# Layer 1's attention scores: the second pass of the query split contracts 64 rows instead of 128, in five PSUM banks at once

## The chip, the cores and the metric

The kernel runs on one core of a Trainium2 chip. The metric is the device time of one execution in microseconds. Before the change the median of three runs is 1772.62 us (1768.93 to 1773.08).

## What is computed

The reference is a two-layer backbone over 1024 latent tokens and 256 context tokens of width 1024. Layer 0 is a latent attention, layer 1 a differential attention. The change lies in layer 1, of which this matters:

```python
q, k, v, gate = project(h, True)          # 8 heads, each with 2 maps of 64 columns
q_c, k_c, v_c, gate_c = project(h_c, False)
...
s = jnp.einsum('bqhgd,bkhd->bhgqk', qb, k).astype(jnp.float32) * scale   # per map; k is latent and context keys, 1280
p = jax.nn.softmax(s, axis=-1).astype(v.dtype)
return jnp.einsum('bhgqk,bkhv->bqhgv', p, v)
...
o = o1 - lam_full.astype(o1.dtype) * o2   # map 0 minus a multiple of map 1
```

Each head has two attention maps, 0 and 1. Each map's scores contract only 64 numbers per query and key. Both maps share the same values of 128 columns.

## The kernel before, in words

Layer 0 and the passage to layer 1 come first and are not touched. Layer 1 runs head after head, eight heads, and within a head over eight tiles of 128 queries. One call of `step1` is one such tile; the text calls it a step and numbers the steps 0 to 63, so step 31 is the last tile of head 3.

TensorE (PE) runs in the order in which the code is written (`manual_schedule` for PE). The orders of VectorE (DVE), ScalarE (ACT), GpSimd (POOL) and the DMA queue (SP) are set by the framework's scheduler from dependences, priorities and its own estimates of time. Every engine works its own list strictly in that order.

One step issues on PE: the scores of its tile (`scores1`), then, in slices between the rest, projections for the next head (`some(side, ...)`, lines 186 to 188), the product with the values of the tile two steps back (`values1`, lines 1392 to 1394), and transposes of the joined map of the tile one step back (`turn1`, line 1384) in three groups of four, four and two.

The numbers are fp32 split in two fp16 parts, high and low. For each map m, `KS[m]` holds 128 rows: the 64 rows of the key's high part and below them the 64 rows of its low part. `QS[m]` holds the query's high part twice, one copy under the other, so one matmul over 128 rows gives (high key + low key) times high query. `Q1[m]` holds the query's low part twice in the same way, and a second matmul over 128 rows adds (high key + low key) times low query. So a block of 512 scores takes two matmuls of 512 columns, lines 1348 and 1349.

`scores1` handles five banks of PSUM in turn: first the context block, where 256 columns of map 0 and 256 of map 1 share a bank; then two blocks of 512 for map 0; then, after a slice of projections, two blocks of 512 for map 1. All of layer 1's PSUM is one ring of eight banks (tag "b"), given out in the order of the code: a bank is written again when the tile that had it eight grants earlier has been read.

What follows a step's scores outside PE:

- DVE reduces each bank to a row maximum: line 1361 the context bank, line 1365 each block of 512. Line 1367 combines three of them to the negative maximum of a map, `mx`. It is needed before any exponential of that map.
- ACT takes the exponentials, three per map (line 1371: 512, 512 and 256 columns), from PSUM to `p0` or `p1`, with the row sums in `sm`. `p0` has two buffers, `p1` one.
- DVE adds the sums (line 1374), forms the factor (1375, 1376) and joins the maps, `p0 + factor * p1` over 1280 columns (line 1377).
- In the next step PE transposes the joined map, ACT writes the high part of it (`ph`, line 182) and DVE the low part (`pl`, line 183).

`prod_k1` and `prod_q1` make the next head's keys and queries. Their tails (`fin`) split the numbers and move them by SP's DMA queue into the 64-row halves of `KS`, `QS` and `Q1`: for a head four transfers for the keys, and eight for each of the two halves of the queries. `wx`, `wy`, `uw`, `kH` and `kL` in the traces belong to this preparation of the next head.

The last head (steps 56 to 63) has no next head to prepare; its slices are filled with the output projection of the layer.

Of the kernel before, what the change touches and what calls it, by code (L numbers as in the profile page):

```python
# [11 lines left out]
F16 = mybir.dt.float16  # L12
# [42 lines left out]
def hybrid_kernel(  # L55
# [30 lines left out]
    def dmv(dst, src):  # L86
        sp.dma_start(dst, src)
# [962 lines left out]
    with ow_ctx, spool("o0") as op0:  # L1050
# [96 lines left out]
        for t in range(8):  # L1147
# [48 lines left out]
            "pl": ([P, NT, P], F16, 2), "KS0": ([P, NTOK], F16, 2), "KS1": ([P, NTOK], F16, 2),  # L1196
            "QS0": ([P, SEQ], F16, 2), "QS1": ([P, SEQ], F16, 2), "Q10": ([P, SEQ], F16, 2),
            "Q11": ([P, SEQ], F16, 2), "vh": ([P, NT, P], F16, 2), "vl": ([P, NT, P], F16, 2),
            "o1": ([P, P], F32, 3), "o2": ([P, P], F32, 2), "mx": ([P, 8], F32, 2), "sm": ([P, 8], F32, 4),
# [6 lines left out]
    TAGO = {"res": ([P, D], F32, 2), "z": ([P, D], F32, 2), "gb3": ([P, D], F32, 1),  # L1206
            "bs": ([P, 2, 6], F32, 2), "mv": ([P, 4], F32, 2)}
    for k_, v_ in TAGL.items():
        rot(wl, v_[0], v_[1], k_, v_[2], first=True)
# [38 lines left out]
    def prod_k1(h, made=()):  # L1248
# [14 lines left out]
        def fin():  # L1263
            H, L = w1("kH"), w1("kL")
            split16(H, L, kr, kc1)
            for m in range(2):
                r = slice(m * HD, m * HD + HD)
                dmv(ks[m][:HD, :], H[r, :])
                dmv(ks[m][HD:, :], L[r, :])

# [3 lines left out]
    def prod_q1(h, b, ps=None):  # L1274
# [64 lines left out]
    def scores1(h, t):  # L1339
# [6 lines left out]

        def st_of(out, m, c0, n):
            pe.matmul(out, qs[m][:, ts], ks[m][:, c0:c0 + n], start=True, stop=False)  # L1348
            pe.matmul(out, q1[m][:, ts], ks[m][:, c0:c0 + n], start=False, stop=True)  # L1349

        st = {}

        def chunk(c0, ms):
            n = 512 // len(ms)
            st[c0, ms] = b = bank("b")
            for i, m in enumerate(ms):
                st_of(b[:, i * n:(i + 1) * n], m, c0, n)
            return b

        b = chunk(SEQ, (0, 1))  # L1360
        dve.tensor_reduce(mx[:, 0:2], b.rearrange("p (a b) -> p a b", a=2), axis=AX.X, op=ALU.max, negate=True)  # L1361
        for m in range(2):
            for i, c0 in enumerate((0, 512)):
                b = chunk(c0, (m,))
                dve.tensor_reduce(mx[:, 2 + 2 * m + i:3 + 2 * m + i], b, axis=AX.X, op=ALU.max, negate=True)  # L1365
            nb = mx[:, 6 + m:7 + m]
            dve.tensor_scalar(nb, mx[:, 2 * m + 2:2 * m + 3], mx[:, 2 * m + 3:2 * m + 4], mx[:, m:m + 1],  # L1367
                              op0=ALU.min, op1=ALU.min)
            for i, (c0, n, b) in enumerate(((0, 512, st[0, (m,)]), (512, 512, st[512, (m,)]),
                                            (SEQ, CTX, st[SEQ, (0, 1)][:, m * CTX:(m + 1) * CTX]))):  # L1370
                act.activation(p[m][:, c0:c0 + n], b, AF.Exp, bias=nb,  # L1371
                               accum_out=sm[:, 2 + 3 * m + i:3 + 3 * m + i])
            yield
# [344 lines left out]
```

## Time and profile before

| What | Value |
|---|---|
| runs, device time | 1773.08, 1772.62, 1768.93 us; median 1772.62 us |
| profiled execution, span from first to last instruction | 1767.7 us (its own device time is not among the numbers; the three runs lie 1.3 to 5.4 us above this span) |
| mean granted TensorE clock | 0.993 |
| busy in the span | PE 94%, weight loads 70%, DVE 69%, ACT 63%, POOL 46% |
| layer 1's steps 0 to 56, 947.70 to 1606.31 us | PE busy 623.01, DVE 521.04, ACT 460.95, POOL 221.44 of 658.61 us |
| PE's first scores, line 1348 | 947.6 us |
| scores on PE, 947 to 1720 us | line 1348 126.5 us, line 1349 129.7 us busy, 384 matmuls each |

How to read it: a busy share is an average; an engine that is busy 94% of the time need not be the one that others wait for. So the chain of waits is read beside it: the view that goes back from the last instruction, at each step to whatever released it. A matmul's row begins when it is issued and includes the time until its last result is written, so rows of consecutive matmuls overlap, and the distance from one start to the next is what a matmul takes from PE.

### The profile page before, as it was taken

What the parts mean: (1) busy time and instruction counts of PE and PEld (TensorE: products, weight loads), DVE (VectorE), ACT (ScalarE), POOL (GpSimd) and SP (SyncE); (2) the same over time, 40 slices, a digit from 0 to 9 for tenths busy, and PEclk for the clock granted to TensorE, in tenths of its full rate; (3) what the DMA queues carried; (4) which work ended last, traced back from release to release, by engine and by line L of the source; (5) the groups of instructions that cost most, each with busy time, mean ns of one, the idle gap of its engine ahead of it and who ended that gap; (6) DMA issues with size and microseconds to landing.
All of it is one profiled execution on the core that took longest, in us unless ns stands there. A gap on an engine that the chain in (4) does not pass through costs nothing. (4 is left out here: it accounts for less than half of the span.)

```text
span 1767.7 us, 36788 instructions
## 1 busy us (share of the span) xinstructions
PE 1660.4 (94%) x14564; PEld 1231.8 (70%) x14564; DVE 1224.6 (69%) x2037; ACT 1118.5 (63%) x2235; POOL 821.9 (46%) x740
## 2 busy tenths in 40 slices
PE   7999989999999998899999999999999999987998
PEld 6999956556666655577867676767676767666876
DVE  7658666565565666646856778787878787878664
ACT  3551177777777778845635676767676767758542
POOL 1432147667767776845552323241424233354454
PEclk9999999999999999999999999999999999999999
DMA  8258520110111122245522222231212222142331
GB/s 308 81 152 259 166 68 21 43 44 22 42 46 25 39 57 62 65 168 196 167 96 64 80 68 80 67 81 55 60 51 63 60 58 75 32 125 66 112 108 72
DMA packets 111225, 154.84 MB, mean 88 GB/s; under 512 B 13415, under 2 KB 84679, under 8 KB 111054
## 3 DMA queue, kind: packets, MB, share of 16 engines
q1 hardware_dynamic: 102654, 144.90, 27.3%
q10 hardware_dynamic: 8400, 7.61, 1.3%
q8 instruction: 114, 1.87, 0.4%
q14 instruction: 57, 0.47, 0.1%
HBM read 98.65 MB, written 27.07 MB: 71 GB/s over the span
## 5 line engine op out<-in xcount | busy, mean ns | idle before, releaser
L780 POOL TENSOR_TENSOR pl<-p,ph 128x1024 f16<-128x1024 f32 (+1 forms) x176 | 364.3, 2076 | 148.4 <-ACT ph L779 122.6
L1371 ACT ACTIVATE p<-ps_b,mx 128x512 f32<-128x512 f32 (+1 forms) x384 | 230.2, 617 | 58.9 <-DVE mx L1367 57.4
L778 ACT ACTIVATE p<-ps_a,esc 128x1024 f32<-128x1024 f32 (+1 forms) x176 | 189.0, 1074 | 94.8 <-PE ps_a L836 88.8
L760 DVE TENSOR_REDUCE mx<-ps_a 128x1 f32<-128x1024 f32 x128 | 155.3, 1222 | 129.9 <-PE ps_a L758 129.8
L779 ACT CAST ph<-p 128x1024 f16<-128x1024 f32 (+1 forms) x176 | 177.1, 1006 | 5.5
L1365 DVE TENSOR_REDUCE mx<-ps_b 128x1 f32<-128x512 f32 x256 | 164.9, 680 | 0.7 <-PE ps_b L1349 0.7
L849 PE MATMUL ps_d<-Vh,pl 128*128 128x65 f16 x1344 | 146.0, 194 | 4.4 <-POOL pl L780 4.4
L846 PE MATMUL ps_d<-Vh,ph 128*128 128x65 f16 x1344 | 148.2, 195 | 0.0
L848 PE MATMUL ps_d<-Vl,ph 128*128 128x64 f16 x1344 | 147.0, 193 | 0.0
L846 PEld LDWEIGHTS <-ph 128*128 128x128 f16 x1344 | 123.3, 97 | 18.1 <-issue 4.9
L848 PEld LDWEIGHTS <-ph 128*128 128x128 f16 x1344 | 124.0, 98 | 12.2 <-issue 0.3
L1348 PE MATMUL ps_b<-KS,QS 128*128 128x512 f16 (+1 forms) x384 | 126.5, 347 | 5.9 <-DVE pl L183 2.9
L1349 PE MATMUL ps_b<-KS,Q 128*128 128x512 f16 (+1 forms) x384 | 129.7, 347 | 0.0
L834 PE MATMUL ps_a<-qH,KH 100*128 100x512 f16 x320 | 121.9, 381 | 7.8 <-ACT p L778 3.5
L1396 POOL TENSOR_TENSOR sm<-sm,us 128x1 f32<-128x1 f32 x64 | 18.5, 289 | 234.3 <-DVE sm L1375 221.2
L849 PEld LDWEIGHTS <-pl 128*128 128x128 f16 x1344 | 123.2, 97 | 5.8 <-POOL pl L780 5.8
L1384 PE MATMUL ps_b<-idr,p 128*128 128x128 f32 x640 | 103.8, 278 | 24.2 <-ACT p L1371 6.2
L183 DVE SCALAR_TENSOR_TENSOR pl<-ps_b,lcf,ph 128x512 f16<-128x512 f32 (+1 forms) x192 | 116.9, 653 | 11.2 <-ACT ph L182 11.2
L182 ACT ACTIVATE ph<-ps_b,lcf 128x512 f16<-128x512 f32 (+1 forms) x192 | 115.2, 647 | 13.9 <-PE ps_b L1384 13.8
L835 PE MATMUL ps_a<-qH,KL 96*128 96x512 f16 x320 | 121.8, 381 | 0.0
L836 PE MATMUL ps_a<-qL,KH 96*128 96x512 f16 x320 | 121.2, 379 | 0.0
L1384 PEld LDWEIGHTS ps_b<-idr,p 128*128 128x128 f32 x640 | 78.2, 143 | 49.0 <-ACT p L1371 11.6
(438 smaller groups left out, 5290.7 us busy)
## 6 DMA issues: line engine op xcount, KB each, us to landing
ws<-in_dw SPq DMA_DIRECT2D x28, 512.0 KB, 3.9
adw<-in_ada_w SPq DMA_DIRECT2D x24, 512.0 KB, 4.6
adaw<-in_ada_w SPq DMA_DIRECT2D x16, 512.0 KB, 7.3
g<-sg_d SPq DMA_DIRECT2D x16, 512.0 KB, 8.5
sg_d<-gg ACTq DMA_DIRECT2D x40, 128.0 KB, 3.6
o_d<-op SPq DMA_DIRECT2D x7, 640.0 KB, 3.8
xt<-in_xT SPq DMA_DIRECT2D x16, 256.0 KB, 4.4
wgs<-in_w_in SPq DMA_DIRECT2D x32, 128.0 KB, 3.1
```

Source lines behind the costliest of these rows:

```text
L760: dve.tensor_reduce(mx[:, t, 0:1], ps, axis=AX.X, op=ALU.max)
L778: act.activation(p32[:, :n], st, AF.Exp, scale=esc0)
L779: act.copy(ph[:, :n], p32[:, :n])
L780: pool.tensor_tensor(pl[:, :n], p32[:, :n], ph[:, :n], op=ALU.subtract)
L846: pe.matmul(pv[:, t, :], ph[:, ts], Vh[:, k, h, :], start=(k == kcs[0] and t == 0), stop=False, skip_group_check=True)
L848: pe.matmul(pv[:, t, :V0], ph[:, ts], Vl[:, k, h, :], start=False, stop=False, skip_group_check=True)
L849: pe.matmul(pv[:, t, :], pl[:, ts], Vh[:, k, h, :], start=False, stop=(k == NT - 1), skip_group_check=True)
L1348: pe.matmul(out, qs[m][:, ts], ks[m][:, c0:c0 + n], start=True, stop=False)
L1349: pe.matmul(out, q1[m][:, ts], ks[m][:, c0:c0 + n], start=False, stop=True)
L1365: dve.tensor_reduce(mx[:, 2 + 2 * m + i:3 + 2 * m + i], b, axis=AX.X, op=ALU.max, negate=True)
L1371: act.activation(p[m][:, c0:c0 + n], b, AF.Exp, bias=nb, accum_out=sm[:, 2 + 3 * m + i:3 + 3 * m + i])
L1384: pe.transpose(st[:, j * P:(j + 1) * P], pc[:, (k0 + j) * P:(k0 + j + 1) * P], idn)
```

## The change

The low part of the query is kept once, as one tile of 128 rows (`QL`, map 0 in rows 0 to 63, map 1 in rows 64 to 127), in place of two copies for each map. The second pass contracts 64 rows: low query times high key only. The product of low query and low key, of the size of the split's own rounding, is left out. To make the rows meet, `KS[1]` now has its low part above and its high part below. Map 0's second matmul then uses rows 0 to 63 of the array, map 1's rows 64 to 127, and the two follow each other, each into its own bank.

For the context block a second form of the high key (`kctx`, one per head in turn) is kept: 512 columns, map 0's keys in the upper left, map 1's in the lower right, zeros elsewhere. One matmul of 512 columns with `QL` gives both maps' low-query products for the context.

To have pairs, `scores1` first issues the first pass of all blocks, into all five banks, then the four second passes; map 1's block comes first in each pair. The slice of projections that stood between map 0 and map 1 now comes after all scores. The maxima and exponentials are written in the code in the same grouping as before, with the context bank's maximum behind map 0's two. The transfers of the low query are gone (four for each half of a head's queries), its split writes `QL` directly, and two transfers per head fill `kctx`, which POOL zeroes once before layer 1.

```diff
-            "QS0": ([P, SEQ], F16, 2), "QS1": ([P, SEQ], F16, 2), "Q10": ([P, SEQ], F16, 2),
-            "Q11": ([P, SEQ], F16, 2), "vh": ([P, NT, P], F16, 2), "vl": ([P, NT, P], F16, 2),
+            "QS0": ([P, SEQ], F16, 2), "QS1": ([P, SEQ], F16, 2), "QL": ([P, SEQ], F16, 2), "vh": ([P, NT, P], F16, 2), "vl": ([P, NT, P], F16, 2),
...
+    kctx = [wl.tile([P, 2 * CTX], F16, name=f"kctx{i}") for i in range(2)]
+    for x in kctx:
+        pool.memset(x, 0.0)
...
             for m in range(2):
                 r = slice(m * HD, m * HD + HD)
-                dmv(ks[m][:HD, :], H[r, :])
-                dmv(ks[m][HD:, :], L[r, :])
+                o = slice(HD - m * HD, 2 * HD - m * HD)
+                dmv(ks[m][r, :], H[r, :])
+                dmv(ks[m][o, :], L[r, :])
+                dmv(kctx[h % 2][r, m * CTX:(m + 1) * CTX], H[r, SEQ:])
...
-            qt1[h] = [w1(f"Q1{m}") for m in range(2)], [w1(f"QS{m}") for m in range(2)]
+            qt1[h] = w1("QL"), [w1(f"QS{m}") for m in range(2)]
...
-            H, L = w1("kH")[:, :n], w1("kL")[:, :n]
+            H, L = w1("kH")[:, :n], q1[:, c]
...
-                dmv(q1[m][:HD, c], L[r, :])
-                dmv(q1[m][HD:, c], L[r, :])
...
-        def st_of(out, m, c0, n):
-            pe.matmul(out, qs[m][:, ts], ks[m][:, c0:c0 + n], start=True, stop=False)
-            pe.matmul(out, q1[m][:, ts], ks[m][:, c0:c0 + n], start=False, stop=True)
...
-        b = chunk(SEQ, (0, 1))
-        dve.tensor_reduce(mx[:, 0:2], b.rearrange("p (a b) -> p a b", a=2), axis=AX.X, op=ALU.max, negate=True)
+        def first(out, m, c0, n):
+            pe.matmul(out, qs[m][:, ts], ks[m][:, c0:c0 + n], start=c0 < SEQ, stop=c0 == SEQ, skip_group_check=True)
+
+        def second(out, m, c0, n):
+            r = slice(m * HD, m * HD + HD)
+            pe.matmul(out, q1[r, ts], ks[m][r, c0:c0 + n], start=False, stop=True, skip_group_check=True)
+
+        b = bank("b")
+        st = {(m, SEQ): b[:, m * CTX:(m + 1) * CTX] for m in range(2)}
+        pe.matmul(b, q1[:, ts], kctx[h % 2], start=True, stop=False, skip_group_check=True)
+        for m in range(2):
+            first(st[m, SEQ], m, SEQ, CTX)
+        for c0 in (0, 512):
+            for m in range(2):
+                st[m, c0] = bank("b")
+                first(st[m, c0], m, c0, 512)
+        for c0 in (0, 512):
+            for m in (1, 0):
+                second(st[m, c0], m, c0, 512)
         for m in range(2):
             for i, c0 in enumerate((0, 512)):
-                b = chunk(c0, (m,))
-                dve.tensor_reduce(mx[:, 2 + 2 * m + i:3 + 2 * m + i], b, axis=AX.X, op=ALU.max, negate=True)
+                dve.tensor_reduce(mx[:, 2 + 2 * m + i:3 + 2 * m + i], st[m, c0], axis=AX.X, op=ALU.max, negate=True)
+            if m == 0:
+                dve.tensor_reduce(mx[:, 0:2], b.rearrange("p (a b) -> p a b", a=2), axis=AX.X, op=ALU.max, negate=True)
             nb = mx[:, 6 + m:7 + m]
...
-            for i, (c0, n, b) in enumerate(((0, 512, st[0, (m,)]), (512, 512, st[512, (m,)]),
-                                            (SEQ, CTX, st[SEQ, (0, 1)][:, m * CTX:(m + 1) * CTX]))):
-                act.activation(p[m][:, c0:c0 + n], b, AF.Exp, bias=nb,
+            for i, (c0, n) in enumerate(CHUNKS):
+                act.activation(p[m][:, c0:c0 + n], st[m, c0], AF.Exp, bias=nb,
```

The added code shifts line numbers: the first passes are line 1350 in the changed kernel, the second passes line 1354, the context matmul line 1358, the maxima lines 1370 and 1372, the negative maximum line 1374, the exponentials line 1377, the sums and the join lines 1380 to 1383.

How PE's order moves is shown for step 31. In the names `ps_b` is a bank, `KS0` and `KS1` are the keys of the two maps, `QS` the high query, `Q10` the low query of map 0. Before, PE issues for map 0's two blocks, and what follows them:

```order
L1348 LDWEIGHTS QS0_2396_15894
L1348 MATMUL ps_b_2720_17920<-KS0_2377_15781,QS0_2396_15894 128x512
L1349 LDWEIGHTS Q10_2394_15892
L1349 MATMUL ps_b_2720_17920<-KS0_2377_15781,Q10_2394_15892 128x512
L1348 LDWEIGHTS QS0_2396_15894
L1348 MATMUL ps_b_2721_17924<-KS0_2377_15781,QS0_2396_15894 128x512
L1349 LDWEIGHTS Q10_2394_15892
L1349 MATMUL ps_b_2721_17924<-KS0_2377_15781,Q10_2394_15892 128x512
L186 LDWEIGHTS h1H_11336
L186 MATMUL ps_b_2722_17934<-wx_2596_17162,h1H_11336 128x256
```

After, the last two first passes and the four second passes of the same step stand like this:

```order
L1350 LDWEIGHTS QS0_2385_15850
L1350 MATMUL ps_b_2706_17849<-KS0_2369_15744,QS0_2385_15850 128x512
L1350 LDWEIGHTS QS1_2386_15851
L1350 MATMUL ps_b_2707_17851<-KS1_2370_15745,QS1_2386_15851 128x512
L1354 LDWEIGHTS QL_2384_15849
L1354 MATMUL ps_b_2705_17847<-KS1_2370_15745,QL_2384_15849 128x512
L1354 LDWEIGHTS QL_2384_15849
L1354 MATMUL ps_b_2704_17845<-KS0_2369_15744,QL_2384_15849 128x512
L1354 LDWEIGHTS QL_2384_15849
L1354 MATMUL ps_b_2707_17851<-KS1_2370_15745,QL_2384_15849 128x512
L1354 LDWEIGHTS QL_2384_15849
L1354 MATMUL ps_b_2706_17849<-KS0_2369_15744,QL_2384_15849 128x512
```

A bank was finished by the matmul right behind its first; now each block waits for its second pass behind all first passes, and the projections of line 186 come after the four second passes.

DVE's order moves with it, since the scheduler places the maxima anew. In step 31, `pl` is the low part of the tile one step back, `mx` the maxima. Before:

```order
L183 SCALAR_TENSOR_TENSOR pl_2708_17847<-ps_b_2714_17895,lcf_87,ph_2707_17846 128x256
L1361 TENSOR_REDUCE mx_2715_17910<-ps_b_2719_17914 128x2
L1365 TENSOR_REDUCE mx_2715_17910<-ps_b_2720_17920 128x1
L1365 TENSOR_REDUCE mx_2715_17910<-ps_b_2721_17924 128x1
L1367 TENSOR_SCALAR mx_2715_17910<-mx_2715_17910 128x1
L1365 TENSOR_REDUCE mx_2715_17910<-ps_b_2723_17947 128x1
L1365 TENSOR_REDUCE mx_2715_17910<-ps_b_2724_17951 128x1
L1367 TENSOR_SCALAR mx_2715_17910<-mx_2715_17910 128x1
L1374 TENSOR_REDUCE sm_2716_17911<-sm_2716_17911 128x2
```

After:

```order
L1372 TENSOR_REDUCE mx_2699_17837<-ps_b_2703_17841 128x2
L183 SCALAR_TENSOR_TENSOR pl_2692_17774<-ps_b_2698_17822,lcf_87,ph_2691_17773 128x256
L1370 TENSOR_REDUCE mx_2699_17837<-ps_b_2705_17847 128x1
L1370 TENSOR_REDUCE mx_2699_17837<-ps_b_2704_17845 128x1
L1370 TENSOR_REDUCE mx_2699_17837<-ps_b_2706_17849 128x1
L1370 TENSOR_REDUCE mx_2699_17837<-ps_b_2707_17851 128x1
L1374 TENSOR_SCALAR mx_2699_17837<-mx_2699_17837 128x1 x2
L1380 TENSOR_REDUCE sm_2700_17838<-sm_2700_17838 128x2
```

The first negative maximum stood behind three maxima; now both stand behind all five.

In step 33, the second tile of head 4, `p0` with two sources is the join of the step before. Before:

```order
L1361 TENSOR_REDUCE mx_2761_18216<-ps_b_2765_18220 128x2
L1376 SCALAR_TENSOR_TENSOR sm_2737_18074<-sm_2737_18074,nlam_86 128x1
L1365 TENSOR_REDUCE mx_2761_18216<-ps_b_2766_18226 128x1
L1377 SCALAR_TENSOR_TENSOR p0_2738_18075<-p1_2739_18076,sm_2737_18074,p0_2738_18075 128x1280
L1365 TENSOR_REDUCE mx_2761_18216<-ps_b_2768_18244 128x1
L1365 TENSOR_REDUCE mx_2761_18216<-ps_b_2767_18230 128x1
L1365 TENSOR_REDUCE mx_2761_18216<-ps_b_2769_18248 128x1
L1367 TENSOR_SCALAR mx_2761_18216<-mx_2761_18216 128x1 x2
```

After:

```order
L1372 TENSOR_REDUCE mx_2745_18141<-ps_b_2749_18145 128x2
L1381 RECIPROCAL sm_2721_18000<-sm_2721_18000 128x2
L1370 TENSOR_REDUCE mx_2745_18141<-ps_b_2751_18151 128x1
L1382 SCALAR_TENSOR_TENSOR sm_2721_18000<-sm_2721_18000,nlam_86 128x1
L1370 TENSOR_REDUCE mx_2745_18141<-ps_b_2753_18155 128x1
L1383 SCALAR_TENSOR_TENSOR p0_2722_18001<-p1_2723_18002,sm_2721_18000,p0_2722_18001 128x1280
L1374 TENSOR_SCALAR mx_2745_18141<-mx_2745_18141 128x1
L1370 TENSOR_REDUCE mx_2745_18141<-ps_b_2750_18149 128x1
L1370 TENSOR_REDUCE mx_2745_18141<-ps_b_2752_18153 128x1
```

Map 1's two maxima now come first, and its negative maximum stands right behind the join, ahead of map 0's maxima.

More of the change, by code (lines that the diff above doesn't have):

```diff
@@ L1345, in scores1 @@
         p = [w1("p0"), w1("p1")]
-        def st_of(out, m, c0, n):
[L1348 to L1358, printed above, removed]
-        b = chunk(SEQ, (0, 1))
-        dve.tensor_reduce(mx[:, 0:2], b.rearrange("p (a b) -> p a b", a=2), axis=AX.X, op=ALU.max, negate=True)
+        def first(out, m, c0, n):
[15 more added lines that the diff above has]
+                second(st[m, c0], m, c0, 512)
         for m in range(2):
             for i, c0 in enumerate((0, 512)):
-                b = chunk(c0, (m,))
-                dve.tensor_reduce(mx[:, 2 + 2 * m + i:3 + 2 * m + i], b, axis=AX.X, op=ALU.max, negate=True)
+                dve.tensor_reduce(mx[:, 2 + 2 * m + i:3 + 2 * m + i], st[m, c0], axis=AX.X, op=ALU.max, negate=True)
+            if m == 0:
+                dve.tensor_reduce(mx[:, 0:2], b.rearrange("p (a b) -> p a b", a=2), axis=AX.X, op=ALU.max, negate=True)
             nb = mx[:, 6 + m:7 + m]
```

## The prediction

> **What bounds the kernel now.** I read the page first, then the busy times of single stretches, then the chain of waits in layer 1, then who waited on DVE, then the order of time around one step.
>
> ```profile
> span 1767.7 us, 36788 instructions
> PE 1660.4 (94%) x14564; PEld 1231.8 (70%) x14564; DVE 1224.6 (69%) x2037; ACT 1118.5 (63%) x2235; POOL 821.9 (46%) x740
> ```
>
> By the page PE is the bound, and the change takes time from PE. The busy times of two stretches are more exact: one head from the sums of step 28 to those of step 36, and four steps of the last head. Columns: length, then busy PE, weight loads, DVE, ACT, POOL.
>
> ```profile
> 1287.79:1380.86 93.07, 90.81 (x786) 67.55 (x785) 74.54 (x146) 67.27 (x184) 33.68 (x48) 1.00 0.20 55
> 1646.58:1714.42 67.84, 67.84 (x434) 53.78 (x433) 45.30 (x93) 34.21 (x88) 34.86 (x36) 1.00 0.37 121
> ```
>
> In the last head PE never rests. In the head before it rests 93.07 − 90.81 = 2.3 us. That looks like PE there too, but the chain of waits says otherwise. This is step 31, whole, from one sum of rows (line 1374) to the next:
>
> ```profile
> 1310.32 0.17 DVE sm L1374
> ...
> 1310.97 1.55 DVE p L1377
> 1312.52 1.71 DVE pl L183 x3
> 1314.23 0.60 DVE mx L1361
> 1314.83 1.21 DVE mx L1365 x2
> ...
> 1316.06 0.28 DVE mx L1367
> ...
> 1316.37 1.56 ACT p L1371 x5
> ...
> 1318.06 2.01 ACT p L1371 x7
> 1320.09 0.17 DVE sm L1374
> ```
>
> There is no PE in it. DVE joins the step before, writes three `pl`, takes three maxima and the negative maximum; ACT takes the exponentials; DVE can go on only when the last one is there. The loop closes after 9.77 us without a gap, and the next step begins from its end. DVE's waits over 600 us of layer 1 (total us, times, longest) agree:
>
> ```profile
> DVE sm L1374 <- ACT p L1371: 88.7, 46, 6.7
> ...
> DVE mx L1365 <- PE ps_b L1349: 0.3, 1, 0.3
> ```
>
> DVE waited 88.7 us for ACT's last exponentials and 0.3 us for PE's scores. So in heads 0 to 6 the loop between DVE and ACT sets the pace, and PE, almost full, runs ahead of it and is held by the ring of banks. In head 7 PE sets it.
>
> **What the second pass saves on PE.** Step 31's scores on PE, and one weight load:
>
> ```profile
> 1311.89 0.27 PE L1348 MATMUL ps_b<-KS,QS 128*128 128x256 f16 x1
> 1311.89 0.10 PEld L1349 LDWEIGHTS <-Q 128*128 128x128 f16 x1
> 1312.00 0.27 PE L1349 MATMUL ps_b<-KS,Q 128*128 128x256 f16 x1
> ...
> 1312.33 0.38 PE L1348 MATMUL ps_b<-KS,QS 128*128 128x512 f16 x1
> 1312.54 0.38 PE L1349 MATMUL ps_b<-KS,Q 128*128 128x512 f16 x1
> ...
> 1313.19 0.27 PE L186 MATMUL ps_b<-wx,h1H 128*128 128x256 f16 x1
> ```
>
> From 1311.89 four matmuls of 256 columns take 0.44 us, 0.11 each; from 1312.33 four of 512 take 0.86 us, 0.215 each. The context costs the same after: one of 512 and two of 256, 0.215 + 0.22 = 0.44. The first passes cost the same, 4 x 0.215. Of the old second passes 4 x 0.215 = 0.86 us per step is at stake. If two halves of the array work at once, two pairs take 2 x 0.215 = 0.43. If they follow each other, it stays 0.86: no row of before shows two matmuls at once, so 0.43 and 0.86 are the bounds. I take 0.43, plus 0.05 because the second of a pair needs its own weights: the load row shows that PE already does a load beside a running matmul, and the two halves share neither rows nor banks.
>
> The Trainium skill, "TensorE: Matmul & The Clock Gate", Part 3, has small tiles in different row groups run at the same time, about 4 ns apart; no row here shows it, and by it the sum below would be 0.05 us per step lower.
>
> Changing from the full array to 64 rows and back is not in the trace, but one place changes to 32 rows:
>
> ```profile
> 125.09 0.40 PE L419 MATMUL ps_c<-u,onr 128*128 128x512 f32 x1
> 125.41 0.18 PEld L465 LDWEIGHTS ps_c<-idr,vm 32*128 32x128 f32 x1 [0.37 <-issue]
> ...
> 125.75 0.19 PEld L186 LDWEIGHTS ps_d<-wgH,hH 128*128 128x128 f32 x1
> 125.75 0.38 PE L186 MATMUL ps_d<-wgH,hH 128*128 128x256 f32 x1
> ...
> 125.97 0.28 PE L187 MATMUL ps_d<-wgL,hH 128*128 128x256 f32 x1
> ```
>
> Line 419's matmul starts at 125.09. Otherwise the next weights load beside it, as at 1311.89. Here the load of the 32-row weights waits 0.37 us for nothing that the profile names, until 125.41, about 0.1 after the 0.215 of a 512-column matmul are over and 0.08 before that row's end. So the array is emptied first, and the load itself, 0.10 for fp16, is no longer hidden: 0.2 us. On the way back the first matmul's row is 0.38 instead of 0.28, the same open load of 0.10, and I take 0.2 again. A round trip is 0.4 us; bounds 0 (the hold has another cause) and 0.5.
>
> Per step: −0.86 + 0.43 + 0.05 + 0.4 = +0.02 us. On PE the change is worth nothing by this sum; between its bounds it is −0.43 (halves overlap, free switch) to +0.4 (no overlap, full switch).
>
> The Trainium skill, "TensorE: Matmul & The Clock Gate", Part 3, also says that a weight load overlaps a running matmul only when the row group differs. The load at 1311.89, in the rows of the matmul that starts with it, speaks against that; by the rule each pair's second use of a half would wait for its load, some 0.1 us per step more.
>
> Where would this be seen? In head 7, at once: 8 x 0.02, nothing. In heads 0 to 6 PE's 2.3 us of rest and its lead come first.
>
> **Later scores.** First passes still end 1.30 us after a step's start (1311.89 to 1313.19), but no block of 512 is finished then; the first comes at 1.30 + 0.2 + 0.215 = 1.7 us plus the 0.16 by which a row outlasts its 0.215. Before, map 0's first was issued by 0.87. DVE begins its maxima 1314.23 − 1311.89 = 2.3 us after the start in step 31, so it does not notice. It is nearest in step 29:
>
> ```profile
> 1290.05 0.27 PE L1348 MATMUL ps_b<-KS,QS 128*128 128x256 f16 x1
> ...
> 1291.70 0.60 DVE mx L1361
> ```
>
> 1.65 us: here DVE, which now asks for a block of 512 first, waits 1.9 − 1.65, about 0.3 us.
>
> **The order of maxima on DVE.** This moves the loop itself. In step 31 both negative maxima now stand behind all five maxima. Exponentials start two maxima (1.21) and one small instruction (0.2) later, and the last ends as much later: +1.4 us. Step 30 has the same new order, but ACT is still casting weights when map 0's maximum is ready:
>
> ```profile
> 1305.66 1.04 ACT wy L182
> 1306.70 3.22 ACT p L1371 x11
> ```
>
> I take +0.3 there (bounds 0 and 1.4). Step 33 goes the other way:
>
> ```profile
> 1335.56 0.59 DVE mx L1361
> ...
> 1336.88 1.98 DVE p L1377
> 1338.86 1.80 DVE mx L1365 x3
> 1340.66 0.19 DVE mx L1367
> ...
> 1340.87 3.70 ACT p L1371 x12
> ```
>
> Between the join and the first negative maximum stood three maxima, 1.80 us; now one more precedes the join and none follows it. The first exponentials start 1.2 us earlier: −1.2 (bounds −1.2 and 0, since ACT now has a `ph` between its exponentials there). Steps 32, 34, 35 and 36 keep the length of their loop by the order. Per head +0.3 + 0.3 + 1.4 − 1.2 = +0.8 us; bounds −1.2 (step 31's delay is caught up in the steps behind it) and +2.0 (step 33 gains nothing). Times seven heads: +5.6, bounds −8 and +14.
>
> **At nothing.** Per head eight transfers of the low query go and two for `kctx` come, on SP, off the chain shown; the scores of a head need them a whole phase later. POOL's two clearings of `kctx` precede its first rope of layer 1, before which it sits idle:
>
> ```profile
> 929.46 1.27 POOL L1245 TENSOR_TENSOR rsw<-rsw,sinB 128x512 f32<-128x512 f32 x1 [4.50 <-DVE rsw L1243]
> ```
>
> 4.5 us cover two instructions of at most 1.3 (that row's length for as many elements in fp32); uncovered they cost 2.6, once. Waits for a fifth bank at once: before, three of the five stood ahead of the projections; the other two now ask 1.1 us earlier for banks that `pl` releases, so PE may be held some 0.5 us per step. In heads 0 to 6 that is taken from its rest; nothing.
>
> Sum: 0 on PE, +5.6 on the loop. The profiled span is 1767.7, its own device time is not given, the three runs lie 1.3 to 5.4 above it; what is summed is a difference and goes on the median: 1772.6 + 5.6 = 1778.
>
> **Rivals.**
>
> *Switching is free and PE sets the pace everywhere.* For it: PE is busy 97.6% of the head shown. Against it: no PE in the loop, and the hold at 125.41. It would save 64 x 0.43 = 27.5 us: 1745. It decides as soon as the round trip costs under 0.43; each 0.1 less is 6.4 us. Chance 0.12.
>
> *The new order gains on the whole.* Step 33's early maximum and `pl`s moved into ACT's time in steps 32 and 33 count, step 31's delay is caught up: −1.2 per head, −8.4: 1764. For it: DVE's waits for ACT, 88.7 us, are what a better order uses. Chance 0.14.
>
> *The halves do not overlap (slower).* Then the second pass costs 0.86 + 0.4: PE pays 0.4 per step, 3.2 per head. Its rest of 2.3 takes most, 0.9 is left, on top of the loop's 0.8; head 7 pays 3.2 in full: 7 x 1.7 + 3.2 = 15: 1788. Against it: separate rows and banks. It decides from a rest below 3.2 per head on. Chance 0.20.
>
> *Nothing reaches the path.* PE breaks even and the loop's shifts cancel: 1773. Chance 0.14.
>
> **How the numbers follow.** My forecast, 1778, has 0.40, with 1766 to 1788 as its own range. About 0.3%, 5.3 us, is what a measurement of this kernel tells from no change. The forecast case gives slower 0.20, same 0.18, faster 0.02; the free switch faster 0.12; the better order faster 0.10, same 0.04; no overlap slower 0.20; the last faster 0.02, same 0.10, slower 0.02. Together faster 0.26, same 0.32, slower 0.42. For 8 in 10 the range takes in the better order's bound and part of the free switch below (1752), no overlap above with the loop's own upper bound in part (1794).
>
> **What would show it.** In the changed trace, matmuls of line 1354 should start in pairs some 0.05 us apart, two pairs 0.215 apart; if four starts lie 0.215 apart, the halves do not overlap. The first of them should start about 0.4 after the last first pass instead of 0.215, and its weight load should show an idle time that nothing explains. The chain in heads 2 to 6 should hold no PE, and the loop of step 31 should last about 11.2 us, not 9.77. Head 7's four steps should still take 67.8 us. A chain that goes through line 1354, or a shorter head 7, would make the prediction wrong.

## The result, and the profile after

The changed kernel takes 1788.92 us (median of four, 1788.02 to 1791.08) where the kernel before takes 1772.49 in the same comparison: 16.4 us more between the medians, a ratio of 1.0109 (95% interval 1.0093 to 1.0124). It is slower, as forecast, and inside the range; but the forecast gave 5.6 us, and the loss is nearly three times that. So the terms need checking one by one.

The page's first lines, and the same two stretches as in the prediction: one head from the sums of step 28 to those of step 36, and four steps of the last head.

```profile
span 1786.5 us, 36551 instructions
PE 1655.7 (93%) x14500; PEld 1202.8 (67%) x14500; DVE 1225.2 (69%) x2037; ACT 1121.4 (63%) x2235; POOL 834.2 (47%) x742
```

```profile
1299.21:1395.07 95.86, 89.55 (x766) 62.33 (x764) 74.49 (x146) 66.23 (x182) 33.45 (x48) 1.00 0.19 53
1665.96:1733.38 67.42, 67.42 (x429) 51.63 (x429) 44.86 (x93) 34.26 (x88) 34.51 (x36) 1.00 0.38 122
```

The profiled span grew by 18.8 us, 2.4 more than the medians differ: the profiled execution of before was a quick one. (The changed kernel's lasted 1788.33 us with a span of 1786.5; with the same 1.8 on top, an estimate, that of before lasted some 1769.5.) DVE and ACT have the same work as before (1224.6 and 1118.5 us then). PE has less. The head shown is 2.8 us longer, and PE's rest in it has grown from 2.3 to 95.86 − 89.55 = 6.3 us. The last head's four steps, which PE sets, are 0.4 us shorter. So the loss lies in heads 0 to 6, and it is waiting. From the first sum of rows (step 0) to the last of head 6 (step 55) before took 645.4 us and after 664.5.

First the second passes themselves. These are PE's rows of step 31's end (the idle time before a row stands in brackets); the second fence is what PE had in hand in 1325.36 to 1325.39 and in 1325.75 to 1325.88.

```profile
1325.05 0.38 PE L1350 MATMUL ps_b<-KS,QS 128*128 128x512 f16 x1 [0.55 <-DVE pl L183]
1325.35 0.61 PE L1354 MATMUL ps_b<-KS,QL 64*128 64x512 f16 x4
1325.89 0.28 PE L186 MATMUL ps_b<-wx,h1H 128*128 128x256 f16 x1
```

```profile
1325.35 0.39 PE L1354 MATMUL ps_b<-KS,QL 64*128 64x512 f16 x2
...
1325.58 0.38 PE L1354 MATMUL ps_b<-KS,QL 64*128 64x512 f16 x2
```

Two second passes together fill 0.39 us, and the row of a single one is 0.38 to 0.39 too: the two halves run side by side, their starts 1 to 7 ns apart in all 64 steps. The next pair starts 0.23 later. The last first pass starts at 1325.05 and the first pair 0.30 later instead of 0.215; the projection starts 0.31 after the second pair instead of 0.215. So a change of form costs 0.09 us, twice a step. From the last first pass to the projection it is 0.84 us here and 0.847 in the median step; before it was 0.215 + 0.86 = 1.075. PE saves 0.23 us a step. (The Trainium skill, "TensorE: Matmul & The Clock Gate", Part 3, has such tiles start about 4 ns apart: the trace agrees.)

The chain of waits through step 31, from one sum (now line 1380) to the next:

```profile
1322.13 0.17 DVE sm L1380
...
1322.78 1.55 DVE p L1383
1324.33 1.32 DVE pl L183 x2
1325.65 0.60 DVE mx L1372
1326.25 0.39 DVE pl L183
1326.64 2.39 DVE mx L1370 x4
1329.03 0.19 DVE mx L1374
...
1329.25 1.61 ACT p L1377 x5
...
1331.16 1.80 ACT p L1377 x7
...
1332.98 0.17 DVE sm L1380
```

It is still the loop of DVE and ACT without PE, and it lasts 10.85 us in place of 9.77: all five maxima stand ahead of the first exponential. Step 32 is longer by 1.65 us for another reason. DVE's rows at its end, after, and then before:

```profile
1343.69 0.75 DVE L183 SCALAR_TENSOR_TENSOR pl<-ps_b,lcf,ph 128x512 f16<-128x512 f32 x1 [1.86 <-ACT ph L182]
...
1344.69 0.73 DVE L1245 STREAM_SHUFFLE rsw<-ps_b 128x512 f32<-128x512 f32 x1
1345.31 0.68 DVE L1246 TENSOR_TENSOR kr<-ps_b,cosB 128x512 f32<-128x512 f32 x1
1345.90 1.14 DVE L183 SCALAR_TENSOR_TENSOR pl<-ps_b,lcf,ph 128x512 f16<-128x512 f32 x2
1346.95 0.15 DVE L1380 TENSOR_REDUCE sm<-sm 128x2 f32<-128x6 f32 x1
```

```profile
1332.40 0.16 DVE L1374 TENSOR_REDUCE sm<-sm 128x2 f32<-128x6 f32 x1 [3.58 <-ACT p L1371]
...
1332.49 0.73 DVE L1243 STREAM_SHUFFLE rsw<-ps_b 128x512 f32<-128x512 f32 x1
1333.11 1.39 DVE L183 SCALAR_TENSOR_TENSOR pl<-ps_b,lcf,ph 128x512 f16<-128x512 f32 x2
```

Before, the sum came first and the rope (lines 1243, 1244) and the `pl` came behind it. Now three `pl` and the rope stand ahead of the sum. The last exponential of this step ends at 1345.24, and its sum waits until 1346.95.

And PE waits as it did not before. One row of the waits in 1000 to 1600 (us, times, longest):

```profile
PE ps_b L1350 <- DVE pl L183: 23.9, 29, 2.3
```

PE stands 23.9 us in this stretch before a first pass whose bank `pl` has yet to free (27.0 over heads 0 to 6, and 2.9 before; the expectations below have 27.3 and 3.2).

DVE has no more work than before, so the 19.1 us that heads 0 to 6 grew by is time in which DVE waits. Two of its waits in the same stretch grew, after and then before:

```profile
DVE pl L183 <- ACT ph L182: 21.4, 15, 3.3
DVE uw L301 <- POOL uw L1001: 19.8, 12, 2.6
```

```profile
DVE pl L183 <- ACT ph L182: 4.1, 5, 1.5
DVE uw L301 <- POOL uw L1001: 8.9, 12, 1.2
```

Its wait for the last exponentials fell, from 88.7 to 70.9 us. DVE, ACT and POOL work their instructions in a new order here; whether that is the cause is asked below.

That leaves three suspects. Theory A: PE stands before the banks, because it asks for five at once, and all else follows. Theory B: the new order of work on DVE and ACT. Theory C: the half arrays with their changes of form.

### The profile page after: what moved, and what is told of

Same layout as the page of the kernel before. It is cut to its first block, busy times and chain, and to the rows that moved or that the text cites. A ratio compares the mean times of both kernels' runs of the same rounds, so it can differ in the third digit from the quotient of the medians.

```text
span 1786.5 us, 36551 instructions
## 1 busy us (share of the span) xinstructions
PE 1655.7 (93%) x14500; PEld 1202.8 (67%) x14500; DVE 1225.2 (69%) x2037; ACT 1121.4 (63%) x2235; POOL 834.2 (47%) x742
## 5 line engine op out<-in xcount | busy, mean ns | idle before, releaser
L182 ACT ACTIVATE ph<-ps_b,lcf 128x512 f16<-128x512 f32 (+1 forms) x192 | 118.3, 651 | 13.6 <-PE ps_b L1390 13.6
L1402 POOL TENSOR_TENSOR sm<-sm,us 128x1 f32<-128x1 f32 x64 | 14.4, 225 | 237.5 <-DVE sm L1381 237.4
L1350 PE MATMUL ps_b<-KS,QS 128*128 128x512 f16 (+1 forms) x384 | 91.4, 350 | 32.1 <-DVE pl L183 28.6
L1398 PE MATMUL ps_b<-vh,ph 128*128 128x128 f16 x640 | 112.0, 221 | 1.1 <-DVE pl L183 1.1
```

The costliest lines, as they stand in the source:

```text
L182: act.activation(hi, src, AF.Copy, scale=scale)
```

## The experiments

All were timed in five rounds against the kernel before. 0.1% is 1.8 us.

### Five banks at once, and late second passes, both with full arrays

The kernel before, with all banks of a step ahead of the slice:

```diff
         b = chunk(SEQ, (0, 1))
+        for m in range(2):
+            for c0 in (0, 512):
+                chunk(c0, (m,))
...
-                b = chunk(c0, (m,))
```

> The kernel before, with full 128-row second passes each right behind its first, but all five banks of a step's scores written ahead of the slice of projections. Theory A (the loss comes from asking for five banks at once: PE stands before a bank that `pl` of the tile before has yet to free): PE's waits for `pl` ahead of a score matmul, 3.2 us in heads 0 to 6 before and 27.3 after, come up to some 20 us here too, and the time is 1783 to 1795. Theory B (the loss is the new order of maxima on DVE): the banks are finished one by one as before, DVE's order stays nearly as before, 1770 to 1777. Theory C (the 64-row form itself costs): 1770 to 1776.

Measured: 1785.28 us, ratio 1.0090 (1.0077 to 1.0103). Then the same with the second passes behind all first passes:

```diff
...
+        for c0 in (0, 512):
+            for m in range(2):
+                st[c0, (m,)] = bank("b")
+                first(st[c0, (m,)], m, c0, 512)
+        for c0 in (0, 512):
+            for m in (1, 0):
+                second(st[c0, (m,)], m, c0, 512)
...
```

> As the run before, with the four second passes of the blocks of 512 behind all first passes, as in the changed kernel, but with 128 rows and no pairs. So it has the changed kernel's order without its half arrays. Theory A: like the run before, some us more: 1786 to 1800; above the changed kernel by what the pairs save, 0.23 us a step in head 7 (2 us) and some part of 13 us in the heads before. Theory B: the new order of maxima is here, so 1786 to 1793, while the run before stays at 1773. Theory C: 1770 to 1776.

Measured: 1781.14, 1.0066 (1.0052 to 1.0080). Full arrays lose too, where theory C had 1770 to 1776 for both: it falls. The first run is where theory A put it, but the second, which asks for more, loses less, and lies below what A and B named.

### Where the slice stands

The changed kernel with the slice of projections ahead of the scores:

```diff
+            some(side, at[0])
             with tc.high_priority(HP):
                 if cur:
                     S = scores1(*cur)
                     next(S)
-            some(side, at[0])
```

> The changed kernel, with the slice of projections that follows the scores put ahead of them, so that PE works on while `pl` frees the banks. Theory A: PE's waits for `pl` ahead of line 1350 fall from 27.3 us in heads 0 to 6 to under 10, and the time falls to 1770 to 1779. Theory B: the scores come no earlier, the order of maxima stays, 1785 to 1792. Theory C: no difference from the changed kernel, 1787 to 1791.

Measured: 1776.69, 1.0043 (1.0029 to 1.0057). Then three banks ahead of the slice and two behind it:

```diff
         for c0 in (0, 512):
             for m in range(2):
                 st[m, c0] = bank("b")
                 first(st[m, c0], m, c0, 512)
+            if c0 == 0:
+                yield
...
-            yield
+        yield
```

> The changed kernel, with three banks (context and the first block of each map) ahead of the slice and two behind it, followed by the four paired second passes. Banks are asked for as in the kernel before; the half arrays stay; the first finished block comes later by a slice of about 1.2 us. Theory A: PE's waits for `pl` ahead of line 1350 under 10 us in heads 0 to 6, time 1770 to 1780, with DVE waiting some us more for scores. Theory B: 1786 to 1795, as the maxima come all together and later. Theory C: 1787 to 1791.

Measured: 1785.6, 1.0098 (1.0083 to 1.0113). The time of the one fits A, though PE's waits for `pl` ahead of a first pass, 13.6 us in heads 0 to 6, are not under 10; in the other they are 17.8, and its time comes nearest to B. Neither separates them, because the scheduler makes new lists for DVE and ACT each time PE's order changes. The four kernels differ in two things at once.

### The lists exchanged

So the lists were taken out of the scheduler's hands. Each of the next kernels holds, for DVE and ACT in layer 1, a table with another kernel's order, and adds an edge of pure order from each instruction to the next:

```diff
...
+    for c, at in ORDER.items():
+        made_ = [i for i in nc.cur_bb.bb.instructions[mark:] if i.engine == ENG[c]]
...
+        for j, k in zip(at, at[1:]):
+            tc.add_manual_dep(made_[k], made_[j].name,
+                              mybir.DependencyInfo(mybir.DependencyClass.NoSync, mybir.DependencyReason.DATA),
+                              reason="order")
```

POOL's and SP's lists stay the scheduler's. POOL's followed the tables: in layer 1's traces its 406 instructions stand in the order of the kernel that the table was taken from, but for one instruction in the changed kernel with the lists of before; so what is exchanged is in effect POOL's list too. First the kernel before with the lists of the changed one:

> The kernel before, its matmuls and PE's order untouched (128-row second passes, three banks ahead of the slice and two behind it); but in layer 1 DVE and ACT work their instructions in the order in which they stand in the changed kernel. Theory A (PE stands before a bank; the lists follow): 1768 to 1776, no change from the kernel before. Theory B (the loss is in the new order on DVE and ACT): 1783 to 1792, most of the changed kernel's loss, with PE's work as before.

Measured: 1801.27, 1.0176 (1.0159 to 1.0192): PE's work is untouched, and it loses 31 us. Step 31's two sums in its trace, 10.84 us apart:

```profile
1329.07 0.16 DVE L1460 TENSOR_REDUCE sm<-sm 128x2 f32<-128x6 f32 x1 [1.19 <-ACT p L1457]
1339.91 0.16 DVE L1460 TENSOR_REDUCE sm<-sm 128x2 f32<-128x6 f32 x1 [3.58 <-ACT p L1457]
```

Theory A has no room for this. The other half of the exchange, the changed kernel with the lists of before:

> The other half of the exchange: the changed kernel's matmuls and PE order (half arrays, five banks at once), with DVE and ACT in layer 1 in the order of the kernel before. Theory A: PE's waits for `pl` stay at some 20 us or more, 1784 to 1795. Theory B: the loss is gone and what the half arrays save on PE, 0.23 us a step, shows in head 7 at least: 1762 to 1772.

Measured: 1780.68, 1.0065 (1.0052 to 1.0078). Between the two theories: giving the old lists back takes 0.44% off the loss of 1.09%, but 11.5 us stay. Next the first run again, with the old lists, so that PE asks for five banks at once and nothing else differs:

> The first run of the study again (128-row passes, each right behind its first, all five banks ahead of the slice), but with DVE and ACT in the order of the kernel before. Only PE's order differs from the kernel before. Theory A: 1779 to 1788, as in that first run. Theory B: 1767 to 1774.

Measured: 1768.51, 0.9999 (0.9987 to 1.0011). Its step 31 takes 9.78 us, and PE does stand before the banks (us, times, longest in 1000 to 1600):

```profile
1310.79 0.16 DVE L1462 TENSOR_REDUCE sm<-sm 128x2 f32<-128x6 f32 x1 [1.04 <-ACT p L1459]
1320.57 0.16 DVE L1462 TENSOR_REDUCE sm<-sm 128x2 f32<-128x6 f32 x1 [2.26 <-ACT p L1459]
```

```profile
PE ps_b L1434 <- DVE pl L269: 17.0, 14, 1.9
```

Theory A falls: with these lists five banks at once cost nothing. The 16 us of the first run were the lists that the scheduler made for it.

What the half arrays bring: the changed kernel's order and lists, second passes over 128 rows, the other map's half of the low query zero:

```diff
-            pe.matmul(out, q1[r, ts], ks[m][r, c0:c0 + n], start=False, stop=True, skip_group_check=True)
+            pe.matmul(out, q1[m][:, ts], ks[m][:, c0:c0 + n], start=False, stop=True, skip_group_check=True)
...
```

> The changed kernel's PE order and its DVE and ACT lists, but the second passes contract all 128 rows, the other map's half of the low query being zeros, so there are no pairs and no change of the array's form. The context's second pass is two matmuls of 256 columns in place of one of 512. It tells what the half arrays bring by themselves. If they save 0.23 us a step on PE as the trace shows, this run is slower than the changed kernel: by 2 us in head 7 and between 0 and 13 us in the heads before, 1789 to 1803. If the form itself costs (theory C), it is faster: under 1786.

Measured: 1794.10, 1.0141 (1.0125 to 1.0157). The half arrays, with the joint context pass and the transfers that go with them, save some 0.3% here, 5 to 6 us; the two intervals just clear each other.

The mean length of a step over heads 1 to 6, by its place in the head (the distance of the starts of the sum rows in the traces, us; places 4 and 5 are left out):

| step of the head | before | old lists, five banks | changed, old lists | changed | before, new lists | padded, new lists |
|---|---|---|---|---|---|---|
| 0 | 13.29 | 13.30 | 13.34 | 14.73 | 14.73 | 14.81 |
| 1 | 10.76 | 10.63 | 10.63 | 10.15 | 10.65 | 10.11 |
| 2 | 12.70 | 12.86 | 14.04 | 12.68 | 12.34 | 12.87 |
| 3 | 12.79 | 12.95 | 13.49 | 14.30 | 14.18 | 14.28 |
| 6 | 12.22 | 12.15 | 12.78 | 12.57 | 12.89 | 12.39 |
| 7 | 10.60 | 10.59 | 10.60 | 10.86 | 10.86 | 10.85 |

In places 0 and 7 the length goes with the list, to a tenth or so, whatever PE does; in 3 it does so among the new lists. The column "changed, old lists" keeps the old lengths at 0 and 7 and loses at 2, 3 and 6.

### What is left with the old lists

> The second run of the study (128-row passes, all first passes into five banks, then the four second passes) with DVE and ACT in the order of the kernel before. Against the run with five banks and the same lists (no change of time) only the second passes move: no block of 512 is finished before the fifth bank is free. Theory D (with the lists of before, what is left of the loss, 11.5 us, is the late finish of the blocks): 1778 to 1788. Theory E (it is the half arrays or what goes with them, the joint context pass, the changed transfers): 1766 to 1773.

Its edit is that of the second run. Measured: 1783.27, 1.0078 (1.0062 to 1.0094). Theory D: with the old lists, it is the late second passes. By place this run loses at 2 and 3 (14.31 and 13.44 us) and hardly at 6 (12.40). PE's waits for `pl` ahead of a score, first here, then in the changed kernel with the old lists:

```profile
PE ps_b L1434 <- DVE pl L269: 28.3, 28, 2.3
```

```profile
PE ps_b L1436 <- DVE pl L269: 28.6, 28, 2.3
```

28 us in place of 17.0, twice as often. PE now comes to the fifth bank earlier, with its second passes still to do. What stands behind a stand in PE's order comes late with it. In the changed kernel with old lists, two stretches of 3.41 us (length, busy PE, loads, DVE, ACT, POOL, granted clock), and rows of them:

```profile
1159.70:1163.11 3.41, 1.48 (x9) 0.46 (x10) 3.32 (x6) 0.00 (x0) 0.52 (x2) 1.00 0.00 0
1163.11:1166.52 3.41, 3.41 (x22) 2.31 (x20) 2.51 (x9) 1.85 (x2) 0.43 (x2) 0.50 0.03 7
```

```profile
1161.36 0.39 PE L1436 MATMUL ps_b<-KS,QS 128*128 128x512 f16 x1 [2.28 <-DVE pl L269]
...
1164.35 0.63 PE L273 MATMUL ps_b<-h1L,wx 128*128 128x512 f16 x1
...
1167.72 0.38 PE L273 MATMUL ps_b<-h1L,wx 128*128 128x512 f16 x1
```

```profile
1164.16 0.42 DVE L1348 COPY kr<-ps_b 128x256 f32<-128x256 f32 x1 [0.63 <-PE ps_b L274]
```

PE stands 2.28 us, and in the next 3.41 us the granted clock is 0.50: a 512-column matmul takes 0.43 from PE, its row 0.63 instead of 0.38. The projection comes late, and DVE, whose list has the copy of line 1348 ahead of the maxima of the blocks of 512, waits 0.63 us for it. That is step 18, 13.77 us long in place of 12.56. Eleven windows at half clock lie in heads 0 to 6 of this trace, two in that of the five banks with the old lists.

But the half clock is not needed for step 18 to be this long. The run with full arrays, late second passes and the same lists has the same stand (2.27 us) there, no half clock, and the same length. Step 18 in it, and then in the changed kernel with the old lists (columns as above, the granted clock third from the end):

```profile
1159.45:1173.22 13.77, 11.24 (x88) 7.13 (x86) 12.61 (x24) 8.54 (x19) 2.36 (x5) 1.00 0.23 62
```

```profile
1157.95:1171.72 13.77, 11.23 (x78) 6.75 (x77) 12.40 (x24) 8.53 (x19) 2.19 (x5) 0.88 0.25 68
```

In both, the copy starts 6.21 us after the sum with which the step begins, before 5.02. (Part of the delay arises ahead of the stand: the small instruction that forms the factor takes 0.71 and 0.92 us in place of 0.22, and the rows do not say why.) The run with full arrays has four windows at half clock in heads 0 to 6 and still loses 13.8 us. What the two have in common is that DVE waits for PE's projections, which now stand behind the wait for a bank and behind the late second passes. From step 0 to step 55 DVE waits for PE 13.4 us in the kernel before, 19.1 with five banks and the old lists, 32.5 with the late second passes on full arrays, 29.0 in the changed kernel with the old lists. (The 5.7 us from the first to the second cost nothing, so these waits are not the loss one for one.)

The half clock shows at place 6. There four steps of the changed kernel with the old lists (6, 14, 22 and 38) take 13.5 to 13.7 us in place of 12.5, and a window at half clock ends some 3 to 4 us ahead of each; step 46, without one, takes 12.50. With full arrays only step 38 has one, and it takes 13.97. So there such a window goes with 1.0 to 1.5 us, 4.6 us in all in the changed kernel with the old lists.

Whether the stands are the cause was asked by putting the slice ahead of the scores again, the changed kernel with the old lists:

> The changed kernel with the slice of projections ahead of the scores, and with DVE and ACT in the order of the kernel before. With those lists and the scores first it took 1780.7, and PE stood 30 us before banks that `pl` had yet to free; eleven windows of 3.4 us at half clock followed such stands. Theory F (those stands, and the half clock behind them, are what the late second passes cost): with the slice ahead PE stands under 15 us, fewer than five such windows, 1764 to 1773. Theory G (the blocks are simply finished too late for DVE): the scores come later still by a slice, 1778 to 1790.

Measured: 1773.38, 1.0019 (1.0009 to 1.0029), against 1.0065 with the slice behind.

```profile
PE ps_b L1436 <- DVE pl L269: 13.8, 20, 1.3
```

The stands are halved, none is over 1.3 us, four windows at half clock are left, and 8 of the 11.5 us are gone, although the scores are issued later. Theory G falls. It ended 0.4 us above what F named. F's half clock isn't borne out, since the run with full arrays has four such windows too and loses 13.8 us. And the edit does two things: it shortens the stands, and it puts a slice of projections ahead of them. DVE's waits for PE fall to 14.2 us, about what they were in the kernel before, and in the steps at place 2 from step 10 on the copy starts 5.02 us after the sum again. How much each of the two does was not taken apart.

### Two attempts at a better version

Half arrays without late second passes, pairs within a map (as in the changed kernel, low query times low key is left out for these blocks):

```diff
-                dmv(ks[m][:HD, :], H[r, :])
-                dmv(ks[m][HD:, :], L[r, :])
+                dmv(ks[m][:HD, :512], H[r, :512])
+                dmv(ks[m][HD:, :512], L[r, :512])
+                dmv(ks[m][:HD, 512:], L[r, 512:])
+                dmv(ks[m][HD:, 512:], H[r, 512:])
...
+            for c0 in (0, 512):
+                r = slice(HD, P) if c0 else slice(0, HD)
+                pe.matmul(st[c0, (m,)], q1[m][r, ts], ks[m][r, c0:c0 + 512], start=False, stop=True, skip_group_check=True)
```

> The kernel before with its banks, its slice and its DVE and ACT order, but the second passes of a map's two blocks contract 64 rows and run side by side: the columns 512 to 1279 of the keys have the low part above and the high part below, so the first block's second pass uses the upper half, the second block's the lower. Each map's blocks are finished before the slice as before. It needs the change of form four times a step instead of twice. By the trace of the changed kernel a map's two second passes take 0.215 + 2 x 0.093 = 0.40 us instead of 0.43: 0.06 us a step saved. Theory D: 1764 to 1771, and 0.5 us less in head 7's eight steps. Theory E: 1775 or more.

Measured: 1775.62, 1.0029 (1.0017 to 1.0042): neither theory's figure, and no gain. Its PE rows in the last head say why:

```profile
1691.49 0.59 PE L1451 MATMUL ps_b<-KS,QS 128*128 128x512 f16 x2
1692.02 0.39 PE L1454 MATMUL ps_b<-KS,Q 64*128 64x512 f16 x2
1692.34 0.61 PE L1451 MATMUL ps_b<-KS,QS 128*128 128x512 f16 x2
```

A map's two blocks take 1692.34 − 1691.49 = 0.85 us; before they took 0.86. The two changes of form use up what the pair saves. In its profiled execution (1780.37 us, the longest of twelve) a step of the last head takes 17.09 in place of 16.96: a weight load waits up to 0.3 us there for DVE's `wy`, as in the changed kernel below. Heads 0 to 6 take 647.5 us, 2.1 more than before; where that comes from was not found.

The changed kernel with DVE's maxima put back in their old relative order, everything else left to the scheduler:

```diff
+        row = []
+
+        def then(i):
+            if row:
+                tc.add_manual_dep(i.ins, row[-1].ins.name,
+                                  mybir.DependencyInfo(mybir.DependencyClass.NoSync, mybir.DependencyReason.DATA),
+                                  reason="order")
+            row.append(i)
+
+        then(dve.tensor_reduce(mx[:, 0:2], b.rearrange("p (a b) -> p a b", a=2), axis=AX.X, op=ALU.max, negate=True))
...
```

> The changed kernel, with one thing fixed on DVE: in each step the five maxima and the two negative maxima stand in the relative order of the kernel before (context, map 0's two, its negative maximum, map 1's two, its negative maximum); all else is left to the scheduler. If the order of the maxima is what makes the new lists dear, the loop of the last step of a head falls from 10.85 to about 9.8 us and the time to 1774 to 1783. If the rest of the lists matters more (where `pl`, the rope and the low parts stand), 1785 to 1792.

Measured: 1787.70, 1.0100 (1.0080 to 1.0119).

```profile
1314.31 0.16 DVE L1388 TENSOR_REDUCE sm<-sm 128x2 f32<-128x6 f32 x1 [2.26 <-ACT p L1385]
1324.09 0.16 DVE L1388 TENSOR_REDUCE sm<-sm 128x2 f32<-128x6 f32 x1 [2.26 <-ACT p L1385]
```

Step 31 is at 9.78 us again, as it should be if the order of the maxima is what made that step longer; since other instructions moved as well, this run alone does not prove it. For the scheduler moved the rest: the steps at place 6, 12.57 in the changed kernel, take 14.31 here on average. No version tried beats the kernel before.

## Why the prediction came out as it did

**What bounds the kernel.** Right in the main. In heads 0 to 6 DVE and ACT set the pace, and PE's savings show there in part at most. But the head that was read was a clean one. Over steps 16 to 55 the chain of before goes through PE for 45 of 472 us, and after for 49 of 483, of which 3.8 on line 1354 (the prediction had said no PE there). A chain through line 1354 and a shorter head 7 were its own signs of being wrong; both came.

**PE's sum, +0.02 us a step.** The overlap was right, and the 0.05 for the second weights of a pair came to 0.01 (the next pair starts 0.226 later in place of 0.215). The change of form was mis-sized: 0.2 us each way was read from a place with 32 rows and fp32; it is 0.09 for 64 rows in fp16. PE saves 0.23 us a step. In the last head 16.96 us became only 16.87, mostly since a weight load there now waits for DVE (the four steps took 67.42 us, not the 67.8 forecast):

```profile
1715.48 0.19 PEld L188 LDWEIGHTS ps_b<-o,wy 128*128 128x128 f32 x1 [0.28 <-DVE wy L178]
```

With the maxima in row the step takes 16.71, the full saving.

**Later scores, +0.3 in step 29.** Nothing: 10.25 us before and after. The term asked only whether the maxima would wait for the scores. The projections behind the late second passes were not in the sum, and with the lists of before it is these that DVE waits for.

**The order of the maxima.** Right where it was worked out: step 30 +0.4 (forecast +0.3), step 31 +1.07 (+1.4). Step 33 gained 1.57 (1.2), but not by its maxima alone: its `pl` and rope had been done ahead of the sum of step 32, which lost 1.65.

**The step that failed: "Steps 32, 34, 35 and 36 keep the length of their loop by the order. Per head +0.3 + 0.3 + 1.4 − 1.2 = +0.8 us."** Steps 32, 35 and 36 grew by 1.65, 0.87 and 0.50. Only the maxima and the join were followed; the scheduler had also moved `pl`, the rope and the low parts. The lower bound was mis-worked too: with step 31's delay caught up the terms give 0.8 − 1.4 = −0.6 a head, not −1.2. And one head was multiplied by seven, while the heads' own differences run from −0.8 to +6.0. From step 0 to step 55 the sum is +19.1 us, 2.7 a head.

**Waits for a fifth bank, "some 0.5 us per step ... taken from its rest; nothing".** The size was right, 27.0 us over 56 steps is 0.48, but nothing in the prediction works it out, so that is luck. With the old lists it costs nothing by itself, as forecast (0.9999). Together with the late second passes it is no longer nothing, 11.5 to 13.8 us with the old lists, through something that the prediction did not have: the projections behind the stand reach DVE late. The half clock behind a long stand adds to it in some steps.

**The rivals.** "The halves do not overlap" gave 1788, almost the measured time, by a mechanism that is false: they overlap in every step. "Switching is free and PE sets the pace" is false as well.

The forecast of slower, and the range, held; but of the 16.4 us the term that was worked out gave a third.

**The whole.** One way from before to after, with ratios: five banks 0.9999; second passes late 1.0078; half arrays and the joint context pass 1.0065; the scheduler's own lists 1.0109. So about 14 us for the late passes, less 2 for the half arrays (their intervals touch), plus 8 for the lists. It is one way only. Going by the lists first they cost 31 us, presumably because they were made for another order on PE: the parts do not add.

## What to carry to other kernels

Where a scheduler sets the order of some engines, an edit on another engine gives them new lists, and the lists can outweigh the edit: hold them fixed and measure each apart before you credit or blame the edit. A saving on an engine that is not in the loop buys little (PE saved 64 x 0.23 = 14.7 us here, and 2 to 6 us of it showed), while a wait put on it can cost through what stands behind it in that engine's order: ask who needs that, and how early. Look where the saved time would be spent before counting it.

## What the runs showed of the hardware

Two matmuls of 64 rows in the two halves of the array, into two banks, start some 3 ns apart and end within 7 ns of each other. A change between 128 and 64 rows costs 0.09 us each way with fp16 matmuls (0.31 us from start to start in place of 0.215).

PE's clock is granted in windows of 3.41 us on one grid in each trace (in that of the kernel before the half-clock windows at 1188.62, 1284.19 and 1581.15 us lie 28 and 87 windows apart). In the 14 traces, from 945 to 1700 us, a window at full clock in which PE rested over 1.94 us was always followed by one at 0.50, one with a rest under 1.54 us never; between the two both happen. The changed kernel, two neighbouring windows:

```profile
1394.59:1398.00 3.41, 1.27 (x7) 0.48 (x5) 2.82 (x6) 3.35 (x9) 0.19 (x1) 1.00 0.09 27
1398.00:1401.41 3.41, 3.41 (x15) 1.51 (x15) 3.24 (x6) 0.43 (x2) 0.00 (x0) 0.50 0.02 5
```

The Trainium skill, "TensorE: Matmul & The Clock Gate", section "HAM oscillation — how this bites in real kernels", has as its rule no idle gaps over some 3.4 us. Here a rest of about half a window is enough, and the single stand before 1161.36 was 2.28 us: by the measurement the limit is tighter.
